# Attention of a hybrid diffusion trunk: probability transposes emitted in groups of eight, products two blocks behind, query loads on ScalarE's queue

## The chip, the cores and the metric

The kernel runs on one core of a Trainium2 chip. The metric is the device time of one execution in microseconds (us); a version is given by the median of its runs.

## What is computed

The reference is a two-layer trunk over 1024 latent tokens and 256 context tokens of width 1024. Layer 0 mixes with a convolution and a gating unit, layer 1 with attention; each has a SwiGLU feed-forward stage. The change touches only the attention of layer 1: eight query heads in two groups of four, each group sharing one key and value head, 1024 latent plus 256 context keys.

```python
def _attend(q, k, v):
    ...
    def block(qi):
        s = jnp.einsum('bqkgd,bskd->bkgqs', qi, k).astype(jnp.float32) * scale
        p = jax.nn.softmax(s, axis=-1).astype(v.dtype)
        return jnp.einsum('bkgqs,bskd->bqkgd', p, v)
    ...
    q_l = _axial_rope(_proj_q(h_lat, w_q, q_g), tables)
    k_all = jnp.concatenate([k_l, k_c], axis=1)
    v_all = jnp.concatenate([v_l, v_c], axis=1)
    y_lat = _attend(q_l, k_all, v_all) @ w_out
```

## The kernel before, in words

Everything is float32. A product is made from a high part (rounded to the format that TensorE multiplies at full rate) and a low part (the rest): three matmuls for one, lines 90 to 92 (`mm3`: high by high, high by low, low by high). `split` (lines 201 and 202) makes the two parts: ScalarE casts the source to the high part, VectorE subtracts it from the source to give the low part.

The attention runs over 32 units: `units` lists the query tile t (0 to 7, 128 queries), the key/value head kv and the pair p of query heads. For each unit and head:

- `load_q` (line 1008): for t of 4 and more the query tile (high and low, 256 KB each) is read back from the buffer `q_d` in HBM when p is 0. That is so for eight units: 16, 18, 20 to 30. The two loads are issued by SP (SyncE), which carries all other loads and stores too.
- `score_a` and `score_b`: scores against the 256 context keys (`sb`, in PSUM banks of tag `tr`; ScalarE copies it out, line 1018) and against the 1024 latent keys (`sa`, two buffers of two banks); VectorE takes the maxima (lines 1027, 1028), ScalarE the exponentials (lines 1032, 1033).
- `score_c`: GpSimd divides by the sum (line 1041).
- `trans` (line 1047): one block is 256 keys by two heads. Four TensorE transposes go to one `tr` bank, then `split` makes `ph` and its low part (a buffer of tag `u`). A unit has five blocks.
- `pv`: six matmuls of a block with the values, into `po`, which holds a `tr` bank for a whole unit; after the fifth block `split` copies it out to `oT`.

There are four `tr` banks, shared by `trans`, `sb` and `po`, and 61 buffers `u`, which serve the low parts, the query tiles, keys, values and outputs. The loop emits, for block b: its `trans`, then one fifth of the scores of the unit two ahead (`score_piece`; pieces 0 and 2 hold `score_a`, 1 and 3 `score_b`), then `pv` of block b - 1. Every ninth block `resid_bg` loads a piece of the residual, which VectorE multiplies and shifts (lines 1098, 1099), and `resid_store` writes it back (line 1106), both on SP.

The order on each engine is not the loop's order. The framework plays the program through a model of its own and gives each engine its instructions in the order in which they become ready there; on the chip each engine then runs its list strictly in order. Buffers of one tag are handed out in program order: in the built program of the kernel before, the 211 buffers `u` and the 255 banks `tr` of this stage come without one exception in the order of the program text. In that list each of the eight query loads stands right behind the VectorE subtraction of block 0 of the unit two earlier, the last user of `u` before it in the program text.

Of the kernel before, what the change touches and what calls it, by code (L numbers as in the profile page):

```python
# [8 lines left out]
F32 = mybir.dt.float32  # L9
# [19 lines left out]
def hybrid_kernel(ctx: ExitStack, tc: tile.TileContext, A, out):  # L29
    nc = tc.nc  # L30
# [17 lines left out]
    def U(shape, dt):  # L48
        return up.tile(shape, dt, tag="u", name="u")

    def T():
        return tp.tile([P, 512], F32, tag="tt", name="tt", bufs=5)
# [4 lines left out]
    def after(inst, deps):  # L57
        for d in deps:
            tc.add_manual_dep(
                inst.ins, d.ins.name,  # L60
                mybir.DependencyInfo(mybir.DependencyClass.NoSync, mybir.DependencyReason.DATA),
                reason="phase order")
# [26 lines left out]
    def mm3(ps, s, m, first, last, more=False):  # L89
        nc.tensor.matmul(ps, s[0], m[0], start=first, stop=False, skip_group_check=more)  # L90
        nc.tensor.matmul(ps, s[0], m[1], start=False, stop=False, skip_group_check=more)  # L91
        return nc.tensor.matmul(ps, s[1], m[0], start=False, stop=last, skip_group_check=more)  # L92
# [107 lines left out]
    def split(src, hi, lo):  # L200
        nc.scalar.copy(hi, src)  # L201
        return nc.vector.tensor_tensor(out=lo, in0=src, in1=hi.bitcast(F32), op=ALU.subtract)  # L202
# [730 lines left out]
    q_d = dp.tile([8, 2, 2, P, 512], F32, name="q_d")  # L933
    qT = {}
# [64 lines left out]
    NB = NK // 2  # L999
# [3 lines left out]
    def load_q(n):  # L1003
        t, kv, p = units[n]
        if t >= 4 and p == 0:
            qT[t, kv] = (U([P, 512], F32R), U([P, 512], F32R))
            for x in range(2):
                i1 = nc.sync.dma_start(out=qT[t, kv][x].bitcast(F32), in_=q_d[t, kv, x])
                after(i1, [norm[2 * (n - 6)]])

    def score_a(n, h):
        t, kv, p = units[n]
        q = [x[:, (2 * p + h) * P:(2 * p + h + 1) * P] for x in qT[t, kv]]
        pt = ap.tile([P, 1280], F32, tag="pt", name="pt")
        sa = pa.tile([P, 1024], F32, tag="sa", name="sa", bufs=2)
        sb = pa.tile([P, 512], F32, tag="tr", name="tr", bufs=4)
        mm3(sb[:, 0:256], q, kT[kv, 2], True, True)
        nc.scalar.copy(pt[:, 1024:1280], sb[:, 0:256])
        mm3(sa[:, 0:512], q, kT[kv, 0], True, True)
        st[n, h] = (pt, sa, q)  # L1020

    def score_b(n, h):
        t, kv, p = units[n]
        pt, sa, q = st[n, h]
        mm3(sa[:, 512:1024], q, kT[kv, 1], True, True)
        mx = small.tile([P, 2], F32, tag="mx", name="mx", bufs=4)
        nc.vector.tensor_reduce(out=mx[:, 1:2], in_=pt[:, 1024:1280], axis=AX.X, op=ALU.max)
        nc.vector.tensor_reduce(out=mx[:, 0:1], in_=sa, axis=AX.X, op=ALU.max)  # L1028
        nm = small.tile([P, 1], F32, tag="nm", name="nm", bufs=4)
        nc.vector.tensor_scalar(out=nm, in0=mx[:, 0:1], scalar1=mx[:, 1:2], scalar2=-SCALE, op0=ALU.max, op1=ALU.mult)  # L1030
        ss = small.tile([P, 2], F32, tag="ss", name="ss", bufs=4)
        nc.scalar.activation(pt[:, 0:1024], sa, AF.Exp, bias=nm, scale=SCALE, accum_out=ss[:, 0:1])  # L1032
        nc.scalar.activation(pt[:, 1024:1280], pt[:, 1024:1280], AF.Exp, bias=nm, scale=SCALE, accum_out=ss[:, 1:2])
        st[n, h] = (pt, ss)

    def score_c(n, h):
        pt, ss = st[n, h]
        rc = small.tile([P, 1], F32, tag="rc", name="rc", bufs=4)
        nc.vector.tensor_tensor(out=rc, in0=ss[:, 0:1], in1=ss[:, 1:2], op=ALU.add)
        nc.vector.reciprocal(out=rc, in_=rc)  # L1040
        norm.append(nc.gpsimd.tensor_scalar(out=pt, in0=pt, scalar1=rc, scalar2=1.0, op0=ALU.mult, op1=ALU.mult))

    def trans(n, k2):
        tr = pa.tile([P, 512], F32, tag="tr", name="tr", bufs=4)
        for kk in range(2):
            for h in range(2):
                nc.tensor.transpose(tr[:, kk * 256 + h * P:kk * 256 + (h + 1) * P],  # L1047
                                    st[n, h][0][:, (k2 * 2 + kk) * P:(k2 * 2 + kk + 1) * P], ident)
        ph, pl = ap.tile([P, 512], F32R, tag="ph", name="ph", bufs=NPH), U([P, 512], F32R)
        marks["att"] = split(tr, ph, pl)  # L1050
        st[n, "p", k2] = (ph, pl)

    def pv(n, k2):
        t, kv, p = units[n]
        if k2 == 0:
            st[n, "o"] = pa.tile([P, 512], F32, tag="tr", name="tr", bufs=4)
        po = st[n, "o"]
        ph, pl = st.pop((n, "p", k2))
        for kk in range(2):
            kt = k2 * 2 + kk  # L1060
            v = V[kt]
            cs = slice(kv * P, (kv + 1) * P)
            ms = slice(kk * 256, (kk + 1) * 256)
            mm3(po[:, 0:256], (v[:, 0, cs], v[:, 1, cs]), (ph[:, ms], pl[:, ms]), kt == 0, kt == NK - 1)
        if k2 == NB - 1:
            if p == 0:
                oT[t, kv] = (U([P, 512], F32R), U([P, 512], F32R))
            hi, lo = (x[:, p * 256:(p + 1) * 256] for x in oT[t, kv])
            split(po[:, 0:256], hi, lo)

    LOOK, LAG = 2, 1
    NPH = 8
    N = len(units)

    def score_piece(n, i):
        if not 0 <= n < N:
            return
        if i == 0:
            load_q(n)
            score_a(n, 0)  # L1080
        elif i == 1:
            score_b(n, 0)
        elif i == 2:
            score_a(n, 1)
        elif i == 3:
            score_b(n, 1)
            score_c(n, 0)
        elif i == 4:
            score_c(n, 1)
# [3 lines left out]
    def resid_bg(n):  # L1093
        t, h = divmod(n, 2)
        x = T()
        i1 = nc.sync.dma_start(out=x, in_=xn2_d[t * P:(t + 1) * P, h * 512:(h + 1) * 512])
        after(i1, [marks["att"]])
        nc.vector.tensor_tensor(out=x, in0=x, in1=rows[h][0], op=ALU.mult)
        nc.vector.tensor_tensor(out=x, in0=x, in1=rows[h][1], op=ALU.add)
        held.append((x, t, h))  # L1100

    held = []

    def resid_store():
        x, t, h = held.pop(0)
        nc.sync.dma_start(out=xr_d[t * P:(t + 1) * P, h * 512:(h + 1) * 512], in_=x)

    for n in range(LOOK):
        for i in range(5):
            score_piece(n, i)  # L1110
    for b in range(N * NB + LAG):
        n, k2 = divmod(b, NB)
        if n < N:
            trans(n, k2)
        score_piece(n + LOOK, k2)
        if b >= LAG:
            pv(*divmod(b - LAG, NB))
        if b % 9 == 8 and b // 9 < 16:
            resid_bg(b // 9)
            if len(held) > 1:  # L1120
                resid_store()
    resid_store()
    ppB.__exit__(None, None, None)
    apB.__exit__(None, None, None)
# [126 lines left out]
```

## Time and profile before

| | |
|---|---|
| median of 3 runs | 2629.03 us (2627.96 to 2629.47) |
| the profiled execution: time | 2629.6 us |
| its span on the engines | 2627.7 us |
| attention blocks (first `trans` to last `pv`) | 1516.23 to 1831.36 us |

All times of the trace count from the start of the span. In a timeline row the columns are start, duration, engine, line, operation, out<-in, and in brackets the idle time before it with what ended it; "xN" is a merged run of N. A window row gives the stretch, its length, the busy time of each engine and then the granted share of TensorE's clock (1.00 is 2.4 GHz, 0.50 is 1.2 GHz).

### The profile page before, as it was taken

Reading aid. Unit: us, or ns where it says so; the run is one execution under the profiler, and the core shown is the slowest. Engines: PE = TensorE matmul, PEld = TensorE weight load, DVE = VectorE, ACT = ScalarE, POOL = GpSimd, SP = SyncE. Lnnn points to the kernel's source line nnn. Section 1 sums busy time; section 2 is a strip of 40 time slices with the busy share of each in tenths; the row PEclk is TensorE's granted clock in tenths of the full one; section 3 lists DMA queues with packets and bytes.
Section 4 is the critical chain, followed back from the end, with each engine's and each line's share of the span. In section 5 each row is a group of like instructions: output and inputs, shape, how many; then the busy total and the mean of one; then the engine's idle time right before and its main releaser. Section 6 shows DMA issues by size and latency. Waiting matters only on the chain. (4 is left out here: it accounts for less than half of the span.)

```text
span 2627.7 us, 34744 instructions
## 1 busy us (share of the span) xinstructions
PE 2541.2 (97%) x12956; PEld 2138.1 (81%) x12956; DVE 1851.3 (70%) x3162; ACT 933.4 (36%) x1656; POOL 326.2 (12%) x254
## 2 busy tenths in 40 slices
PE   8999999999999999989999999999989999999997
PEld 6778888787788888879988789888868888888885
DVE  3888488999866655687759488777688665663267
ACT  1311145323233323164433277666163333342220
POOL 0132000112200020010006332222001000000001
PEclk9999999999999999989999999999999999999998
DMA  8453155344422753266541100113324222243232
GB/s 242 144 186 110 57 168 171 118 160 141 129 81 83 268 175 110 91 227 195 183 141 52 41 29 25 65 41 102 131 73 144 81 81 89 80 168 133 68 117 77
DMA packets 156106, 313.68 MB, mean 119 GB/s; under 512 B 25696, under 2 KB 45152, under 8 KB 155936
## 3 DMA queue, kind: packets, MB, share of 16 engines
q1 hardware_dynamic: 155936, 311.46, 36.1%
q8 instruction: 102, 1.67, 0.3%
q14 instruction: 68, 0.56, 0.1%
HBM read 262.05 MB, written 49.35 MB: 119 GB/s over the span
## 5 line engine op out<-in xcount | busy, mean ns | idle before, releaser
L90 PE MATMUL mm<-u,w 128*128 128x512 f32 x1232 | 480.6, 392 | 11.9 <-DVE m L591 4.5
L91 PE MATMUL mm<-u,w 128*128 128x512 f32 x1232 | 482.8, 392 | 3.8 <-DVE u L202 2.8
L92 PE MATMUL mm<-u,w 128*128 128x512 f32 x1232 | 476.7, 391 | 1.9 <-DVE w L202 1.9
L90 PE MATMUL mm<-w,u 128*128 128x512 f32 x832 | 322.7, 392 | 5.8 <-ACT u L201 3.0
L91 PE MATMUL mm<-w,u 128*128 128x512 f32 x832 | 324.3, 390 | 0.0
L92 PE MATMUL mm<-w,u 128*128 128x512 f32 x832 | 321.5, 390 | 0.0
L201 ACT CAST w<-sw 128x512 fp32r<-128x512 f32 x264 | 163.2, 622 | 419.7 <-PE mm L91 365.9
L202 DVE TENSOR_TENSOR w<-sw,w 128x512 fp32r<-128x512 f32 x264 | 191.1, 728 | 169.8 <-ACT w L201 138.5
L90 PEld LDWEIGHTS mm<-u,w 128*128 128x128 f32 x1232 | 232.8, 189 | 64.0 <-DVE m L591 6.4
L91 PEld LDWEIGHTS mm<-u,w 128*128 128x128 f32 x1232 | 232.7, 189 | 53.6 <-DVE u L202 4.6
L92 PEld LDWEIGHTS mm<-u,w 128*128 128x128 f32 x1232 | 232.8, 189 | 50.9 <-DVE w L202 2.6
L90 PE MATMUL mm<-u,hi 128*128 128x256 f32 (+1 forms) x736 | 238.5, 324 | 3.3 <-ACT tt L470 1.8
L84 ACT CAST hi<-wf 128x1024 fp32r<-128x1024 f32 x134 | 138.8, 1050 | 285.3 <-PE mm L91 76.9
L92 PE MATMUL mm<-u,lo 128*128 128x256 f32 (+1 forms) x736 | 237.5, 324 | 0.8 <-DVE lo L86 0.8
L91 PE MATMUL mm<-u,hi 128*128 128x256 f32 (+1 forms) x736 | 237.8, 323 | 0.0
L90 PE MATMUL mm<-hi,u 128*128 128x512 f32 x536 | 209.3, 395 | 3.6 <-DVE tt L917 1.3
L91 PE MATMUL mm<-lo,u 128*128 128x512 f32 x536 | 210.0, 392 | 2.1 <-DVE lo L86 2.1
L92 PE MATMUL mm<-hi,u 128*128 128x512 f32 x536 | 205.7, 393 | 0.0
L86 DVE TENSOR_TENSOR lo<-wf,hi 128x1024 fp32r<-128x1024 f32 x134 | 164.5, 1238 | 43.2 <-ACT hi L84 43.2
L90 PEld LDWEIGHTS mm<-w,u 128*128 128x128 f32 x832 | 157.2, 189 | 39.4 <-ACT u L201 3.9
L92 PEld LDWEIGHTS mm<-w,u 128*128 128x128 f32 x832 | 156.6, 188 | 32.7
L91 PEld LDWEIGHTS mm<-w,u 128*128 128x128 f32 x832 | 156.6, 188 | 32.3
(186 smaller groups left out, 4538.8 us busy)
## 6 DMA issues: line engine op xcount, KB each, us to landing
raw<-in_ffn_in SPq DMA_DIRECT2D x88, 512.0 KB
ad<-in_ada_w SPq DMA_DIRECT2D x112, 256.0 KB
act<-m SPq DMA_DIRECT2D x88, 256.0 KB
raw<-act SPq DMA_DIRECT2D x44, 512.0 KB
sw<-in_ffn_out SPq DMA_DIRECT2D x88, 256.0 KB
wf<-in_ffn_in SPq DMA_DIRECT2D x44, 512.0 KB
wf<-in_w_m SPq DMA_DIRECT2D x32, 512.0 KB
ab<-in_ada_w SPq DMA_DIRECT2D x48, 256.0 KB
```

Source lines behind the costliest of these rows:

```text
L84: nc.scalar.copy(hi, wf)
L86: (lo_eng or nc.vector).tensor_tensor(out=lo, in0=wf, in1=hi.bitcast(F32), op=ALU.subtract)
L90: nc.tensor.matmul(ps, s[0], m[0], start=first, stop=False, skip_group_check=more)
L91: nc.tensor.matmul(ps, s[0], m[1], start=False, stop=False, skip_group_check=more)
L92: return nc.tensor.matmul(ps, s[1], m[0], start=False, stop=last, skip_group_check=more)
L201: nc.scalar.copy(hi, src)
L202: return nc.vector.tensor_tensor(out=lo, in0=src, in1=hi.bitcast(F32), op=ALU.subtract)
```

## The change

Three edits. The query loads are issued by ScalarE instead of SP. The products lag two blocks instead of one. The loop goes by two blocks: first the transposes of both (eight), then for each of the two its score piece and the `pv` of two blocks earlier; the residual calls stay at the same blocks.

```diff
@@ load_q
-                i1 = nc.sync.dma_start(out=qT[t, kv][x].bitcast(F32), in_=q_d[t, kv, x])
+                i1 = nc.scalar.dma_start(out=qT[t, kv][x].bitcast(F32), in_=q_d[t, kv, x])
                 after(i1, [norm[2 * (n - 6)]])
@@ the loop
-    LOOK, LAG = 2, 1
+    LOOK, LAG = 2, 2
...
-    for b in range(N * NB + LAG):
-        n, k2 = divmod(b, NB)
-        if n < N:
-            trans(n, k2)
-        score_piece(n + LOOK, k2)
-        if b >= LAG:
-            pv(*divmod(b - LAG, NB))
-        if b % 9 == 8 and b // 9 < 16:
-            resid_bg(b // 9)
-            if len(held) > 1:
-                resid_store()
+    for b in range(0, N * NB + LAG, 2):
+        for x in range(b, b + 2):
+            if x < N * NB:
+                trans(*divmod(x, NB))
+        for x in range(b, b + 2):
+            n, k2 = divmod(x, NB)
+            score_piece(n + LOOK, k2)
+            if x >= LAG and x - LAG < N * NB:
+                pv(*divmod(x - LAG, NB))
+            if x % 9 == 8 and x // 9 < 16:
+                resid_bg(x // 9)
+                if len(held) > 1:
+                    resid_store()
```

## Rows read from the trace of the kernel before

**Rows 1.** The page, busy time, share of the span and instructions of TensorE and the others

```profile
PE 2541.2 (97%) x12956; PEld 2138.1 (81%) x12956; DVE 1851.3 (70%) x3162; ACT 933.4 (36%) x1656; POOL 326.2 (12%) x254
```

**Rows 2.** Windows: units 0 to 13, units 14 to 29, the last two units

```profile
1516.23:1648.27 132.04, 130.58 (x942) 121.54 (x941) 111.78 (x240) 96.58 (x227) 40.45 (x30) 1.00 0.10 35
1648.27:1816.11 167.84, 157.47 (x1090) 142.32 (x1089) 128.15 (x273) 108.95 (x253) 42.13 (x31) 0.99 0.18 59
1816.11:1831.36 15.25, 14.08 (x114) 13.18 (x112) 8.92 (x19) 9.18 (x21) 2.68 (x2) 1.00 0.09 28
```

**Rows 3.** Timeline of TensorE, neighbours in a stretch without a wait

```profile
1680.77 0.39 PE L90 MATMUL sa<-u 128*128 128x512 f32 x1
1680.99 0.39 PE L91 MATMUL sa<-u 128*128 128x512 f32 x1
...
1682.81 0.28 PE L92 MATMUL tr<-ph,u 128*128 128x256 f32 x1
1682.93 0.28 PE L90 MATMUL tr<-ph,u 128*128 128x256 f32 x1
...
1687.18 1.04 PE L1047 MATMUL tr<-ident,pt 128*128 128x128 f32 x8
```

**Rows 4.** Waits of TensorE in the stage: total us, times, longest us

```profile
PE tr L90 <- DMA u<-q_d: 4.8, 2, 3.4
PE tr L91 <- DVE u L202: 2.6, 7, 0.6
PE tr L90 <- DVE u L202: 2.4, 4, 1.0
```

**Rows 5.** Timeline of SP's queue: query loads, residual load and store

```profile
1674.21 0.88 SPq L1008 DMA_DIRECT2D u<-q_d  x2
...
1712.92 0.42 SPq L1096 DMA_DIRECT2D tt<-xn_d  x1
1730.54 0.32 SPq L1106 DMA_DIRECT2D xr_d<-tt  x1
1730.95 0.88 SPq L1008 DMA_DIRECT2D u<-q_d  x2
...
1753.02 0.88 SPq L1008 DMA_DIRECT2D u<-q_d  x2
```

**Rows 6.** Timeline around the query load of unit 24, TensorE and ScalarE

```profile
1728.41 0.60 PE L1047 MATMUL tr<-ident,pt 128*128 128x128 f32 x4
1728.62 1.12 ACT L1032 ACTIVATE pt<-sa,nm 128x1024 f32<-128x1024 f32 x1 [0.20 <-DVE nm L1030]
...
1730.23 0.57 ACT L201 CAST ph<-tr 128x512 fp32r<-128x512 f32 x1
1730.69 0.38 ACT L201 CAST u<-tr 128x256 fp32r<-128x256 f32 x1
...
1733.71 0.36 PE L90 MATMUL tr<-u 128*128 128x256 f32 x1 [3.40 <-DMA u<-q_d]
```

**Rows 7.** Timeline around the query load of unit 26, ScalarE and TensorE

```profile
1753.16 0.59 ACT L201 CAST ph<-tr 128x512 fp32r<-128x512 f32 x1 [0.91 <-PE tr L1047]
1753.64 1.12 ACT L1032 ACTIVATE pt<-sa,nm 128x1024 f32<-128x1024 f32 x1
...
1755.23 0.37 ACT L201 CAST u<-tr 128x256 fp32r<-128x256 f32 x1
...
1756.28 0.36 PE L90 MATMUL tr<-u 128*128 128x256 f32 x1 [1.41 <-DMA u<-q_d]
```

**Rows 8.** Windows: behind TensorE's idle times of 3.10, 3.40 and 1.41 us

```profile
1505.60:1508.90 3.30, 3.30 (x11) 2.82 (x12) 1.61 (x3) 1.35 (x3) 0.00 (x0) 0.50 0.00 0
1734.30:1737.60 3.30, 3.30 (x17) 3.10 (x15) 0.69 (x1) 0.59 (x1) 0.00 (x0) 0.50 0.07 25
1756.30:1759.70 3.40, 3.40 (x23) 3.05 (x24) 0.69 (x1) 0.97 (x2) 1.04 (x1) 1.00 0.21 78
```

**Rows 9.** Timeline row behind that 3.10 us idle; tile view: durations of query-load issues (ns)

```profile
1505.54 0.69 PE L981 MATMUL tr<-ident,tt 128*128 128x128 f32 x2 [3.10 <-DVE tt L922]
...
L1008 SPq DMA_DIRECT2D u<-q_d x16: 359/394/987, 1642.1 to 1795.9; - x16
```

## Prediction

> **What bounds the kernel now.** I read the page first: TensorE is busy for 97% of the span, VectorE, the next, for 70% [rows 1]. So only TensorE's losses can be won back, and only inside the attention stage that the change touches. Second, the timeline, for TensorE's pace without a wait: a 256-column matmul every 0.12 us, a 512-column one every 0.23 us, a transpose every (1.04 - 0.27)/7 = 0.11 us (the last one's own 0.27 us taken off the run of eight) [rows 3]. A unit has 20 transposes, 36 matmuls of 256 columns (30 of `pv`, 6 of `sb`) and 12 of 512: 20 x 0.11 + 36 x 0.12 + 12 x 0.23 = 9.28 us. Third, the windows. Units 0 to 13 take 132.04 us where the pace gives 14 x 9.28 = 129.9: 2.1 us lost. Units 14 to 29 take 167.84 where it gives 148.5: 19.3 us lost. The last two have no scores left to compute (2 x 5.8 = 11.6) and take 15.25: 3.7 us lost [rows 2]. In all 25.1 us, 1% of the time: more than that the change can't win. Where are the 19.3 us? Beside the blocks of units 14 to 29 stand the eight query loads, two units ahead of their use. Fourth, the waits: 4.8 us for two loads, 5.0 us in 11 waits for the low parts of a block [rows 4], and behind the longest of them 3.3 us at half clock [rows 8], which costs half of it, 1.65 us. The rest is restarts and weight loads that wait for the same things.
>
> **The loads now.** SP issues in order. For unit 20 it issues the pair at 1674.21, well ahead. For unit 24 it can't: its queue stands at the residual's store from 1713.34 to 1730.54, until VectorE has made the data, and the loads follow at 1730.95 [rows 5]. TensorE had run out of work and waits 3.40 us, until 1733.71 [rows 6]. For unit 26 the issue is at 1753.02 [rows 5] and TensorE goes on at 1756.28 after a wait of 1.41 us [rows 7]. From issue to first use that is 2.76 and 3.26 us: the price of a load nobody has asked for in time.
>
> **Part 1, the loads on ScalarE's queue.** Removed: the wait behind the residual's store. Added: two issues on ScalarE, which no row of before shows there; on SP one takes 0.36 to 0.99 us [rows 9]. 16 x 0.39 = 6.2 us of an engine that is busy for 109 us of 168 [rows 2]: nothing by itself. What counts is where in ScalarE's list they stand. Buffers `u` go out in program order, and before the load come the low parts of the two blocks of its group. So in ScalarE's list the load stands behind the casts of both blocks, and these need the group's eight transposes. SP could run ahead of TensorE; ScalarE can't, its casts tie it to TensorE. Count from T, the end of the eight transposes. The first cast can start 0.44 us before T, each takes 0.57 to 0.59 us [rows 6, 7]: the second ends at T + 0.74 at the earliest. 2.76 to 3.26 us later the query is there: T + 3.5 to T + 4.0. TensorE meanwhile has the products of two blocks, 12 x 0.12 = 1.44 us, and then nothing: the next transposes need a `tr` bank, those also go out in program order, and the `sb` that waits for the query comes first. So it stands for 2.1 to 2.6 us. ScalarE also has an exponential of the unit before in its list there: from 1728.62 to the cast at 1730.23 it holds the engine for 1.61 us [rows 6]; at unit 26 it comes right behind the cast and lets the next instruction go only at 1755.23, 2.2 us after SP had issued the load [rows 7]. With it ahead of the load the stand is 3.7 to 4.2 us. I take 3.1, the middle of 2.1 and 4.2, since I can't tell how often it gets ahead. Stands of 3.10 and 3.40 us were both followed by half clock, one of 1.41 us was not [rows 7 to 9]; so I add 1.5 us, nearly the whole 1.65. Eight loads: 8 x (3.1 + 1.5) = 36.8 us lost; from 8 x 2.1 = 16.8 (no half clock) to 8 x (4.2 + 1.65) = 46.8.
>
> The Trainium skill (DMA: Bandwidth & Descriptors, Issuing engines are not separate DMA queues) says that all issuing engines feed the same 16 DMA engines, and that spreading the issues saves only the sequencer's issue time. By that the move would save 0.88 us of SP per pair, on which nobody waits, and change the sum by nothing. The trace differs in one place: the 17 us that SP stands at a store are a wait in an issuing engine's list, and the move ends that one and takes on another.
>
> **Part 2, the lag of two and the groups of eight.** No instruction is added on TensorE, and fewer changes between transposes and matmuls bring nothing by themselves: with ten of them or more in a unit, the 2.1 us that 14 units lose [rows 2] leave at most 0.015 us for each. `pv` of a block now comes behind the transposes of the next group, so cast and subtraction have a whole group, 2 x 9.28/5 = 3.7 us, more; the 5.0 us of waits for low parts [rows 4] and their restarts should go. Against it: two blocks want two of the four `tr` banks at once, with `po` in one and often `sb` in another. Bounds for all losses outside the loads: 2 us (nearly all gone) to 8 us (0.1 us of bank wait in each of 80 groups). I take 4, near the 2.1 us which the first 14 units lose now. The end gains a little: four block products instead of two stand behind the last transposes; that is in the 4.
>
> **The sum.** Lost after: 36.8 + 4 = 40.8 us, against 25.1: +15.7 on the profiled 2629.6 us, 2645.3. The median of the runs is 0.6 lower: 2644.7, say 2645. With the lower bounds (16.8 + 2): 2622.7. With the upper (46.8 + 8): 2658.7.
>
> **Rivals.**
> (a) Faster: the loads get ahead. If ScalarE's list holds them 1.3 us ahead of T or more (2.76 less the fill of 1.44), TensorE never stands for a query, the 4.8 us, the half clock and the drains in front of the loads go, and some 7 us of losses stay: 2629 - 25.1 + 7 = 2611. For it: SP's own issue at 1674.21 shows that the data and buffers are there long before. Against it: the order of the buffers, which had no exception.
> (b) Balance: the stands stay at about 2.3 us, short enough for full clock, 8 x 2.3 = 18.4, and 6 us elsewhere: 24.4 against 25.1, 2628. It is also what the rule on issuing engines comes to, by these rows. For it: the low bound is near; against it: the exponential stood beside the cast in both stretches shown.
> (c) The banks run short on top: a block's bank is free after cast and subtraction, and an exponential ahead makes that 1.6 us later; if a third of the 80 groups waits 0.4 us, 10 us more than the forecast: 2655.
> That the scheduler undoes the grouping is possible (it already emits eight in a row in places [rows 3]); the loads would still stand behind a cast, and the time would be the forecast's.
>
> **How the numbers follow.** Forecast 63%, (a) 13%, (b) 14%, (c) 10%. The range of 2621 to 2659 leaves out (a) and the top of (c) and of the forecast. A measurement of this kernel tells 0.2% (5.3 us) from no change. Faster by more: (a) and the low ends of (b) and the forecast, 16%. Within: most of (b), 14%. Slower: 70%.
>
> **What would show it.** In the profile after, TensorE should wait for the query loads eight times instead of twice, 17 to 34 us in total instead of 4.8, each time with the load issued by ScalarE just behind a cast or an exponential; the granted clock should drop to half behind most of these; and waits of `pv` for low parts should be nearly gone, with units 0 to 13 at 131 us or less. I am wrong if the issues stand several us ahead of their use, or if ScalarE's list has them ahead of the group's casts; and if the waits are there but below 2 us at full clock, it is (b).

## The result and the profile after

| | before | after |
|---|---|---|
| median | 2628.49 us (2627.11 to 2629.47, 4 runs) | 2653.41 us (2652.53 to 2654.28, 4 runs) |
| profiled execution, its span | 2629.6, 2627.7 us | 2652.56, 2650.8 us |
| first `trans` to last `pv` | 1516.23 to 1831.36 = 315.1 us | 1512.06 to 1855.87 = 343.8 us |

The changed kernel is slower: ratio 1.0095, 95% interval 1.0078 to 1.0113, or 24.9 us between the medians. The forecast was 2645 in a range of 2621 to 2659. In the profiled executions the difference is 23.0 us. The attention blocks take 28.7 us more; before them 4.2 us and behind them 1.5 us come off, in code that the change does not touch.

The page of the changed kernel, busy time and the new DMA queue (packets, MB, share of 16 engines):

```profile
PE 2544.3 (96%) x12956; PEld 2140.0 (81%) x12956; DVE 1850.8 (70%) x3162; ACT 932.6 (35%) x1656; POOL 326.4 (12%) x254
...
q10 hardware_dynamic: 2304, 4.20, 0.5%
```

Every engine has as many instructions as in [rows 1]; the loss is in idle time and in the clock. The windows of the same three stretches as in [rows 2] (units 0 to 13, 14 to 29, the last two):

```profile
1512.06:1649.76 137.70, 132.03 (x941) 121.28 (x940) 110.69 (x240) 97.31 (x227) 40.44 (x30) 1.00 0.09 30
1649.76:1841.52 191.76, 164.98 (x1090) 150.05 (x1089) 129.24 (x273) 108.72 (x257) 42.66 (x32) 0.93 0.17 54
1841.52:1855.87 14.35, 13.68 (x114) 13.02 (x112) 8.78 (x18) 7.88 (x17) 2.68 (x2) 1.00 0.09 27
```

The first number behind the colon is the length, the next TensorE's busy time; their difference is its idle time. Units 0 to 13, in which TensorE waits for no query load, take 5.7 us more than before, 4.2 of it idle. Units 14 to 29 take 23.9 us more: idle 26.8 instead of 10.4, and a granted clock of 0.93 instead of 0.99. What TensorE waits for, from 1500 to 1860 (total us, times, longest), as in [rows 4]:

```profile
PE tr L90 <- DMA u<-q_d: 21.3, 8, 3.5
PE tr L90 <- ACT pt L1018: 9.1, 15, 0.7
...
PE tr L90 <- DVE u L202: 1.1, 3, 0.7
...
PE tr L91 <- DVE u L202: 0.3, 1, 0.3
```

The waits for query loads went from 4.8 to 21.3 us and from two to eight. The second row was not there before: 15 waits for the copy of context scores out of their bank. The waits for low parts went from 5.0 to 1.4 us. Now one load, that of unit 20, which before came "well ahead" [rows 5]; TensorE, ScalarE and its queue (ACTq):

```profile
1693.70 1.13 ACT L1032 ACTIVATE pt<-sa,nm 128x1024 f32<-128x1024 f32 x1
...
1694.11 0.66 PE L1047 MATMUL tr<-ident,pt 128*128 128x128 f32 x4
...
1695.29 1.08 ACT L201 CAST ph<-tr 128x512 fp32r<-128x512 f32 x2
...
1695.80 0.28 PE L92 MATMUL tr<-ph,u 128*128 128x256 f32 x1
...
1696.17 0.33 ACTq L1008 DMA_DIRECT2D u<-q_d  x1
1696.24 0.41 ACT L201 CAST u<-tr 128x256 fp32r<-128x256 f32 x1
...
1698.93 0.55 PE L90 MATMUL tr<-u 128*128 128x256 f32 x1 [2.85 <-DMA u<-q_d]
```

The group's transposes end at 1694.77, and the casts of both blocks run from 1695.29 to 1696.37 behind an exponential. TensorE's last product ends at 1696.08, the load goes out at 1696.17, and TensorE, out of work in between, goes on 2.76 us after the issue. The row behind the issue is the cast of an output: the group's products complete `po` of the unit before, and `split` copies it out. In ScalarE's list of the built program seven of the eight loads stand right behind this cast, which waits for TensorE's last product, and these seven go out 0.04 to 0.10 us after that product's end. So TensorE has nothing left when such a load starts. The load of unit 16 stands ahead of that cast:

```profile
1650.32 0.63 PE L1047 MATMUL tr<-ident,pt 128*128 128x128 f32 x4
...
1650.99 0.34 ACTq L1008 DMA_DIRECT2D u<-q_d  x1
...
1651.62 1.08 ACT L201 CAST ph<-tr 128x512 fp32r<-128x512 f32 x2
...
1653.40 0.37 ACT L201 CAST u<-tr 128x256 fp32r<-128x256 f32 x1 [0.70 <-PE tr L92]
...
1653.75 0.36 PE L90 MATMUL tr<-u 128*128 128x256 f32 x1 [0.39 <-DMA u<-q_d]
```

It goes out when the group's transposes end (1650.95), 2.37 us before TensorE runs out of work, and only 0.39 us of wait remain. The granted clock behind the stands (next to last column; the last row is the stretch behind the 2.87 us stand of unit 18):

```profile
1698.64:1702.05 3.41, 3.12 (x13) 2.85 (x13) 0.18 (x1) 0.59 (x1) 0.00 (x0) 0.50 0.57 184
1722.53:1725.95 3.42, 2.93 (x12) 2.66 (x13) 0.12 (x1) 0.42 (x1) 0.00 (x0) 0.50 0.65 210
1746.43:1753.25 6.82, 5.97 (x21) 5.22 (x22) 1.80 (x3) 1.55 (x3) 0.00 (x0) 0.50 0.14 54
1773.73:1777.15 3.42, 3.42 (x15) 3.11 (x14) 1.38 (x2) 1.17 (x2) 0.00 (x0) 0.50 0.02 5
1797.63:1801.04 3.41, 3.35 (x14) 3.08 (x15) 0.23 (x1) 0.59 (x1) 0.00 (x0) 0.50 0.06 25
1821.52:1828.35 6.83, 5.78 (x20) 5.12 (x21) 1.85 (x4) 1.55 (x3) 0.01 (x1) 0.50 0.10 36
1676.40:1679.80 3.40, 3.40 (x22) 3.01 (x23) 1.43 (x3) 1.45 (x3) 0.00 (x0) 1.00 0.45 154
```

TensorE is busy for 24.6 us at half clock, which costs half of that, an estimated 12.3 us; before it was one stretch and 1.7 us [rows 8]. The loads thus cost 21.3 + 12.3 = 33.6 us. The bank wait, in a stretch far from any load:

```profile
1594.98 1.03 PE L1047 MATMUL tr<-ident,pt 128*128 128x128 f32 x8
...
1595.61 1.07 ACT L201 CAST ph<-tr 128x512 fp32r<-128x512 f32 x2
...
1595.77 0.36 PE L90 MATMUL tr<-u 128*128 128x256 f32 x1
...
1596.57 0.39 ACT L1018 COPY pt<-tr 128x256 f32<-128x256 f32 x1
...
1597.01 0.39 PE L90 MATMUL tr<-ph,u 128*128 128x256 f32 x1 [0.65 <-ACT pt L1018]
```

Eight transposes fill two banks; the context scores `sb` (from 1595.77) take another; the next matmul is the first of a new `po`, which gets the bank that `sb` has just filled. ScalarE copies it out only behind both casts, and TensorE stands for 0.65 us. In the built program 15 of the 32 `po` follow an `sb` in their bank as TensorE's very next matmul, which is the number of the waits. (In the kernel before, 8 `po` follow an `sb` in their bank too, but with 16 matmuls or more in between, and none of them waits.) The two counts agree in every version below that has such waits: 13 in e2, 9 in e3, 17 in e4, 4 in e7, 10 in e9.

### The profile page after: what moved, and what is told of

Its sections match the earlier page's. It is cut to its first block, busy times and chain, and to the rows that moved or that the text cites. A ratio compares the mean times of both kernels' runs of the same rounds, so it can differ in the third digit from the quotient of the medians.

```text
span 2650.8 us, 34737 instructions
## 1 busy us (share of the span) xinstructions
PE 2544.3 (96%) x12956; PEld 2140.0 (81%) x12956; DVE 1850.8 (70%) x3162; ACT 932.6 (35%) x1656; POOL 326.4 (12%) x254
```

## The experiments

The theory: the loads' place in ScalarE's list makes most of the loss, and a shortage of `tr` banks the rest; the queue as such costs nothing. All edits keep the whole computation. "Stage" is the stretch from the last transpose ahead of the attention (L981) to the last `pv`, in the profiled execution: 325.1 us before, 352.9 after.

### One part alone

**e1_queue_only**: the kernel before with the loads on ScalarE.

```diff
-                i1 = nc.sync.dma_start(out=qT[t, kv][x].bitcast(F32), in_=q_d[t, kv, x])
+                i1 = nc.scalar.dma_start(out=qT[t, kv][x].bitcast(F32), in_=q_d[t, kv, x])
```

> The loop of before (single blocks, lag of one), only the query loads issued by ScalarE. Theory A (the place of the load in ScalarE's list sets the stand): TensorE waits for the loads at all eight places, 2.5 to 3.4 us each, 20 to 27 us in total instead of 4.8, half clock behind most of them (6 to 13 us of lost work); the bank waits on the copy of line 1018 are not there; 2640 to 2652 us. Rival B (the groups of eight and the lag make the loss, the queue is indifferent): no more than two waits for loads, 2626 to 2632 us.

2642.86 us, ratio 1.0069 (1.0054 to 1.0084); stage 341.5, +16.4. TensorE's waits for the loads and the windows of units 0 to 13 and 14 to 29:

```profile
PE tr L90 <- DMA u<-q_d: 20.0, 8, 3.2
...
1511.14:1643.22 132.08, 130.65 (x943) 121.59 (x942) 111.81 (x240) 96.52 (x227) 40.32 (x30) 1.00 0.09 31
1643.22:1828.45 185.23, 161.69 (x1089) 147.80 (x1088) 127.73 (x273) 108.98 (x254) 42.25 (x31) 0.95 0.17 56
```

One word in the code makes eight waits of 20.0 us in all, and 17.1 us at half clock (8.5 lost) beside them. Units 0 to 13 do not move (132.08 against 132.04). In ScalarE's list six of the eight loads stand behind the output's cast, and TensorE stands 2.70 to 3.19 us for each. Those of units 26 and 30 stand ahead of it and cost 1.27 and 1.26 us. Unit 26:

```profile
1759.02 0.33 ACTq L1008 DMA_DIRECT2D u<-q_d  x1
...
1760.91 0.38 ACT L201 CAST u<-tr 128x256 fp32r<-128x256 f32 x1
...
1761.85 0.35 PE L90 MATMUL tr<-u 128*128 128x256 f32 x1 [1.27 <-DMA u<-q_d]
```

**e2_groups_only**: the changed kernel with its loads on SP.

```diff
-                i1 = nc.scalar.dma_start(out=qT[t, kv][x].bitcast(F32), in_=q_d[t, kv, x])
+                i1 = nc.sync.dma_start(out=qT[t, kv][x].bitcast(F32), in_=q_d[t, kv, x])
```

> Groups of eight and the lag of two, the query loads back on SP. Theory A: SP issues some of the loads ahead of their use, so the waits for them fall from 21.3 us to 3 to 8 us; what stays of the change is some fifteen waits of 0.6 us for a tr bank; 2626 to 2640 us. Rival B (the groups make the loss): the time stays within 4 us of 2653.

2628.20 us, ratio 1.0009 (1.0000 to 1.0019); stage 326.5, +1.4. The same rows:

```profile
PE tr L90 <- ACT pt L1018: 7.9, 13, 0.7
PE tr L90 <- DMA u<-q_d: 5.3, 4, 2.7
...
1515.18:1652.87 137.69, 132.00 (x941) 121.24 (x940) 110.67 (x240) 97.25 (x227) 40.35 (x30) 1.00 0.10 34
1652.87:1818.25 165.38, 154.72 (x1091) 140.64 (x1089) 126.95 (x273) 108.55 (x257) 42.52 (x32) 0.99 0.18 60
```

Groups and lag lose 5.7 us in units 0 to 13 and win 2.5 in units 14 to 29; in all 0.2% at most. The 5.7 us are the same as in the full change.

**e3_lag_only**: the kernel before with the lag of two.

```diff
-    LOOK, LAG = 2, 1
+    LOOK, LAG = 2, 2
```

> The kernel before with the lag of two and nothing else: single blocks, loads on SP at their old place. Theory A: the bank waits on the copy of line 1018 come from the pairs, so they are not there (at most three); the waits for low parts fall from 5.0 us to under 3; the waits for loads stay at 3 to 8 us; 2620 to 2629 us. Rival E (the lag makes the bank waits, since po starts later): ten or more waits on line 1018, 2629 to 2640 us.

2630.20 us, ratio 1.0004 (0.9994 to 1.0013); stage 326.2. There are 9 bank waits of 5.3 us and 9 low-part waits of 4.5 us, where I had expected at most three of the first and under 3 us of the second. The time, too, lies just above the 2620 to 2629 us of that theory. So the lag alone, with the old loop, already brings bank waits, and low-part waits hardly fall (from 5.0). The order of the text shows why: with a lag of two the first `pv` of a unit is emitted right behind piece 2, which holds an `sb`; with a lag of one it stood behind piece 1, which holds none.

### The loads early

**e6_before_early_load** and **e8_early_on_scalar**: each load called one unit earlier in the program text, so that the `u` buffer that it takes comes free a whole unit before its use; on SP and on ScalarE.

```diff
         if i == 0:
-            load_q(n)
+            if n + 1 < N:
+                load_q(n + 1)
             score_a(n, 0)
```

> The kernel before with the loads (on SP) emitted five blocks earlier, nothing else. Theory A: the 4.8 us of waits for loads and the 1.65 us of half clock go, and so do most of the drained waits in front of the loads, since the scheduler no longer sees TensorE out of work there: 8 to 18 us faster than before, 2610 to 2620 us. Rival C (the waits for low parts come from the lag of one, not from the loads' place): only 5 to 7 us faster, 2621 to 2624 us.

> The loop of before with the loads five blocks earlier, as e6, but issued by ScalarE. Theory A (only the place in the list matters): no wait for a load, the time within 5 us of e6's 2612. Rival D (16 issues in ScalarE's list cost by themselves, by holding the exponentials and casts behind them): 5 us or more slower than e6, with new waits on ScalarE's casts beside the loads.

e6: 2612.25 us, ratio 0.9948 (0.9931 to 0.9965), stage 310.4. e8: 2610.91 us, ratio 0.9937 (0.9922 to 0.9951), stage 309.8. Units 14 to 29 of e6, then of e8, and the issues of e8 (duration in ns, least, median, most):

```profile
1649.31:1802.53 153.22, 149.84 (x1085) 139.29 (x1084) 128.32 (x274) 109.39 (x257) 43.54 (x32) 1.00 0.20 64
```

```profile
1646.95:1800.25 153.30, 150.60 (x1085) 139.56 (x1084) 127.96 (x274) 109.23 (x257) 43.59 (x32) 1.00 0.19 64
...
L1008 ACTq DMA_DIRECT2D u<-q_d x16: 326/338/447, 1639.2 to 1773.7; - x16
```

No wait for a load is left in either, no half clock in units 14 to 29, and the two queues cannot be told apart. This is the rule of the Trainium skill (DMA: Bandwidth & Descriptors, Issuing engines are not separate DMA queues), that all issuing engines feed the same DMA engines: e6 and e8 agree with it to 0.1%. e1, the same edit with the load at its old place, costs 0.7%. So not the queue decides but what stands ahead of the load in its list. Both versions beat both kernels; e8 has the lowest median that was run, with e5 and e6 within its interval.

**e4_change_early_load**: the changed kernel with the same earlier call.

> The whole change, loads on ScalarE, but each pair of loads is emitted with piece 0 of the unit before, five blocks (some 10 us) earlier. Theory A: no wait of TensorE for a query load and no half clock in the stage; the bank waits stay (about fifteen of 0.6 us); 33 us of loss go, 2616 to 2624 us. Rival B (ScalarE's issue itself costs, or the groups): the time stays above 2640 us.

2620.36 us, ratio 0.9981 (0.9971 to 0.9990); stage 320.0. The waits for loads are gone, those for banks are not:

```profile
PE tr L90 <- ACT pt L1018: 10.5, 17, 0.7
```

Between e4 and e8 lie the groups and the lag alone, without a load that waits: 10.1 us of the stage. (In its built program 17 `po` follow an `sb` as the next matmul: again the number of waits.)

**e7_lag_early**: e6 with the lag of two.

> Single blocks, lag of two, loads on SP five blocks earlier: e6 with the lag of two. Theory A: the 2.9 us of waits for low parts left in e6 go, nothing new comes; 2607 to 2613 us. Rival G (the third block in flight runs the tr banks short): new waits on line 1018 or for the transposes, 2614 us or more.

2616.89 us, ratio 0.9956 (0.9941 to 0.9971); stage 315.3, 4.9 more than e6.

```profile
PE tr L90 <- DVE u L202: 6.7, 12, 1.0
...
PE tr L90 <- ACT pt L1018: 2.3, 4, 0.6
```

The lag takes half of those 10 us, here mostly in waits for the subtraction (2.6 us in 3 times in e6), so the forecast that nothing new would come was wrong. That the groups take the other half is a difference between runs, not a run of its own.

**e9_one_group_early**: the changed kernel with each load called at the end of the piece just before its old place.

```diff
         if i == 0:
-            load_q(n)
             score_a(n, 0)
...
             score_c(n, 1)
+            if n + 1 < N:
+                load_q(n + 1)
```

> The whole change, loads on ScalarE, emitted with piece 4 of the unit before: one group of two blocks earlier instead of e4's five blocks. Theory A: they then stand in ScalarE's list behind the casts of the group before, 3 to 4 us earlier, and the waits of 2.8 us were that long; so less than 3 us of waits for loads in all eight together, 2618 to 2625 us. Rival H (the lead must be much longer, since ScalarE's list falls behind TensorE's): waits of 1 us and more at most places, 2630 us or more.

2627.76 us, ratio 1.0004 (0.9994 to 1.0013); stage 325.5. The waits shrink, as the place in the list would have it, but do not quite go: 5.1 us in 7 times, against under 3 that the theory allowed, and the time misses its 2618 to 2625 us.

```profile
PE tr L90 <- ACT pt L1018: 6.1, 10, 0.7
PE tr L90 <- DMA u<-q_d: 3.5, 6, 0.9
...
PE tr L92 <- DMA u<-q_d: 1.6, 1, 1.6
```

No half clock lies in units 14 to 29. The stage is 5.5 us longer than e4's. One piece of head start is not quite enough; a whole unit's is (e4).

### The order within a group

**e5_early_values_first** and **e10_change_values_first**: `pv` emitted ahead of the score piece, so that a new `po` takes its bank before `sb` does; e5 on top of e4, e10 on the changed kernel, loads at their place on ScalarE.

```diff
-            score_piece(n + LOOK, k2)
             if x >= LAG and x - LAG < N * NB:
                 pv(*divmod(x - LAG, NB))
+            score_piece(n + LOOK, k2)
```

> The whole change with the loads five blocks earlier, as e4, and in each group the value products emitted ahead of the score piece of their block, so that po asks for its bank before the sb of that place does. Theory A (po waits for the bank of the sb just ahead of it): the seventeen waits of 0.6 us on the copy of line 1018 go or fall below 3 us, 2608 to 2615 us. Rival F (ScalarE is late anyway, with two casts in a row): waits of the same total turn up on another bank, 2617 us or more.

> The whole change with the loads at their own place on ScalarE, and only the value products emitted ahead of the score piece of their block. Theory A (loads and bank waits are two separate losses that add up): the bank waits on line 1018 fall from 9.1 us to under 3, the eight waits for loads stay at 18 to 25 us in all, 2640 to 2647 us. Rival I (the waits for loads shorten as well, or lengthen by what the bank waits gave up): 2636 us or less, or 2649 us or more.

e5: 2612.51 us, ratio 0.9939 (0.9922 to 0.9955), stage 309.7: no wait for L1018 by a product with values is left, and the 10.3 us that it wins over e4 are what groups and lag had cost. e10: 2633.87 us, ratio 1.0025 (1.0014 to 1.0036), stage 333.5. Its waits and the windows of units 0 to 13 and 14 to 29:

```profile
PE tr L90 <- DMA u<-q_d: 15.9, 8, 3.0
...
1514.38:1646.63 132.25, 130.36 (x942) 120.41 (x941) 111.06 (x239) 95.57 (x226) 39.92 (x30) 1.00 0.09 31
1646.63:1823.11 176.48, 158.65 (x1091) 146.04 (x1089) 132.27 (x277) 110.11 (x257) 43.04 (x33) 0.96 0.19 59
```

Units 0 to 13 are back at 132.25: the 5.7 us there were the order of `sb` and `po`, nothing else. But the whole stage wins 19.4 us, twice the 9.1 us of bank waits, so the theory of two separate losses (2640 to 2647 us) failed and its rival held. In units 14 to 29 three of the eight stands for a load, those of units 18, 20 and 22, shrink to 0.57, 0.57 and 0.66 us, and the loss to half clock there falls from 12.3 to 6.8 us (13.6 us busy at half). Unit 18:

```profile
1671.38 0.33 ACTq L1008 DMA_DIRECT2D u<-q_d  x1
...
1673.63 0.37 ACT L201 CAST u<-tr 128x256 fp32r<-128x256 f32 x1 [0.70 <-PE tr L92]
...
1674.16 0.35 PE L90 MATMUL tr<-u 128*128 128x256 f32 x1 [0.57 <-DMA u<-q_d]
```

From issue to use it is still 2.78 us, so the loads are not quicker; they go out 2.2 us before TensorE runs out of work. The built program shows why: in ScalarE's list just these three loads stand ahead of the output's cast. The other five stand behind it and cost 2.68 to 2.96 us. In the changed kernel, e1 and e10 together, 18 loads stand behind that cast and cost 2.68 to 3.47 us each, and 6 stand ahead of it and cost 0.39 to 1.27 us. No run moves the cast alone.

### The sum of the parts

Lengths against the kernel before, us:

| | units 0 to 13 | 14 to 29 | stage |
|---|---|---|---|
| e1, the queue | 0.0 | +17.4 | +16.4 |
| e2, groups and lag | +5.7 | -2.5 | +1.4 |
| sum | +5.7 | +14.9 | +17.8 |
| after | +5.7 | +23.9 | +27.8 |

Where there are no loads the parts add up; in units 14 to 29 they make 9 us more together. Against before, idle time rises there by 13.2 (e1) and 0.3 (e2), together 13.5, but by 16.4 in the changed kernel; the loss to half clock by 6.8 and 0.0, but by 10.6. That is 6.7 of the 9, and one more load stands behind the output's cast than in e1, seven instead of six; the remaining 2.3 us are busy time that e1 and e2 each save and that the changed kernel saves only once. Why the clock fell in six stretches in the changed kernel, two of them double, against five in e1 is open: no run changes the clock alone.

## Why the prediction was right, and where not

**Direction and main cause: right.** TensorE waits for the query eight times instead of twice, 21.3 us (17 to 34 was forecast), and by e1 the queue edit alone makes it slower, by e8 only through the loads' place.

**Part 1, the loads: right in size, by another path.** Forecast 36.8 us, measured 33.6: stands of 2.76 to 3.47 us in seven cases where I took 3.1, one of 0.39, and 12.3/8 = 1.5 us of half clock for each, as taken. But I had the end of the second cast, or an exponential ahead of the load, set the issue. Neither did: at unit 20 the second cast ended at T + 1.60, with T = 1694.77, and the load was out at T + 1.40; at unit 16 it went out while an exponential still ran, before the group's casts began. That ScalarE's list ties the load to TensorE was right, but what held seven of the loads is an entry that I had not counted, the cast of the output just completed, which waits for TensorE's last product. A stand is then the whole time from issue to use, about what I had priced. That the middle of 2.1 and 4.2 us came so near is in part luck.

**Part 2, the losses outside the loads: the step that failed.** I took 4 us, bounds 2 to 8. By the same pace the units lose 137.70 - 129.9, 191.76 - 148.5 and 14.35 - 11.6 us, 53.8 in all; less 33.6 that is 20.2. Bank waits are 9.1 of them, and emitting `po` first wins 10.3 (e5 against e4). The other half I had expected to shrink with the lag and the groups, and it did not: by the same pace, 290.0 us for all units, e5 still loses 10.5 us (300.5 from first `trans` to last `pv`) and e8 10.7 (300.7), though in both no load is late and no `po` waits. Where these 10 us go was not taken apart. I had seen that four banks would be short, but priced it at the 2.1 us which the first 14 units lost before; they lose 7.8 now ("131 us or less" was wrong, it is 137.70). I had looked at the blocks' banks. It was `po` right behind `sb`, whose copy stands in ScalarE's list behind two casts instead of one. The low-part waits fell as said, from 5.0 to 1.4, but by e3 and e7 the lag of two brings bank waits in their place.

**The sum.** Loads 3.2 us below the forecast, the rest of the units 16.2 above, the code outside the units 5.7 below: 7.3 above the 2645.3 for the profiled execution, which took 2652.56. The time fell in the range, near its upper end, partly by luck: these errors are of both signs.

**The rivals.** (a), the loads ahead, did not occur: no load went out before its group's transposes had ended. (b), balance, did not occur: seven stands were of 2.76 us and more, and half clock followed six of them. (c), banks running short on top, did occur, with 10% the least likely: 15 waits of 0.6 us, in size what it had put at 10 us and 2655, though by another buffer than its own mechanism, a block's bank held by an exponential. The rule of the Trainium skill (DMA: Bandwidth & Descriptors, Issuing engines are not separate DMA queues) holds here for the queue and says nothing of the list; by e1 the place in the list was worth 16.4 us of the stage.

**"More than 25.1 us can't be won"**: e8 wins 17.8 us against its runs of before. Of the 19.3 us that units 14 to 29 lost, 14.5 were the loads: 153.3 us there instead of 167.8.

## What to carry to other kernels

Before moving a DMA to another engine's queue, look up in the built program what stands ahead of it there, and what those entries wait for. The costly entry here was a cast that waits for the last product of the very engine that needs the load; the order of the program text did not show it, since the text has the load ahead of that cast. Look also whether the DMA's buffer could be claimed earlier: one unit earlier was worth 0.5 to 0.6%, on either queue, and the move alone cost 0.7%. When blocks are grouped, list who takes each shared PSUM bank next: a long-lived accumulator that takes the bank of a tile just filled waits for that tile's copy, and here emitting it first cost nothing. Two edits that meet in the same stretch need not add up: here they lost 9 us more together.

## What was not expected of the hardware

ScalarE's queue can issue a DMA before the engine has done, or even begun, what is listed ahead of it. At unit 16 of the changed kernel both of the group's casts stand ahead of the load, which goes out at 1650.99, 0.63 us before the first of them begins; at unit 20 it goes out 0.07 us ahead of the output's cast listed before it (1696.24). In both the load comes just after what the cast nearest ahead of it waits for on TensorE: 0.04 us after the end of the transposes and 0.09 us after the last product. In these rows, then, the list holds a DMA back by that wait, and not by the time that the casts themselves take.

Equal stands did not always end in the same clock: 2.87 us at unit 18 left TensorE at full clock (2.4 GHz), 2.85 us at unit 20 at half (1.2 GHz). In e1 a stand of 3.05 us (unit 16) was followed by full clock and one of 1.26 us (unit 30) by half. The length of the idle time alone does not decide it.
